# A recurrent trunk on one core: the RWKV's four steps written ahead of the HGRN's heads

## Chip, core and metric

The kernel runs on 1 core of one Trainium2 chip. The metric is the device time of one execution in microseconds (us); lower is better.

## What is computed

One layer of a streaming encoder on 256 frames of 1024 features: a layer norm, one wide projection, three mixers on slices of it, a gated merge, a layer norm, a mixture of experts, a layer norm.

```python
feats = h @ w_in
z, xbc, dt_raw, f_rwkv, f_hgrn, gates = _split(feats, IN_SIZES)
y_a = _ssd(z, xbc, dt_raw, ...)
y_b = _rwkv7(f_rwkv, ...)
y_c = _hgrn2(f_hgrn, ...)
merged = (sigmoid(g_a) * (y_a @ w_br_ssd) + sigmoid(g_b) * (y_b @ w_br_rwkv)
          + sigmoid(g_c) * (y_c @ w_br_hgrn))
h = _layernorm(DN_ALPHA * h + merged @ w_out, ln1_g, ln1_b)
h = _layernorm(DN_ALPHA * h + _moe(h, ...), ln2_g, ln2_b)
```

The two mixers of this change are recurrences over the frames. The RWKV-7 keeps a 64 by 64 state for each of 16 heads: `s = s * w_t + (s a_t) b_t + v_t k_t`, and gives `y = s r_t`, which is normed per head. The HGRN2 has 8 heads with a decaying outer-product state, computed in chunks of 64 frames, and a root-mean-square norm per head.

## The kernel before

**Projections.** `feat` (through `stream`, whose products stand on lines 358 to 368) makes 256 columns of `h @ w_in`. It loads two tiles of 512 KB, splits each weight into a high and a low part (`L183` on ScalarE, `L184` on VectorE, four buffers each), and issues 48 products into a PSUM tile `st` of three buffers: `L366` to `L368` with the weights stationary, `L358` to `L360` with the frames stationary. These 48 are called streams here. A stream waits for its split weights and its `st` tile, for nothing else.

**The RWKV.** `rwkv_part` prepares eight pairs of heads in two batches, `s0` (pairs 0 to 3) and `s1` (pairs 4 to 7). `rwkv_solve` inverts small triangular systems on VectorE, 32 times a product `L593` and a sum `L595`, and passes the result through DRAM (`L599`, `L605`). `rwkv_solve_off` completes the inverse: transposes `L618` on VectorE, products `L623`, copies `L627`, products `L631`, copies `L635`. Then four steps follow, each over two pairs of a batch. A step is `rwkv_b`, four rounds, one for each chunk of 64 frames:

```python
nc.tensor.matmul(ch[hs[h], 0, :], sc[:, h, c, 0:64], uv[:, c, h, :], ...)        # L654
nc.tensor.matmul(ch[h, 0, :], ars[h, c - 1, 0:64], z[h, c - 1, h], ...)          # L658
nc.scalar.activation(w, ch[:, 0, :], AF.Copy)                                    # L660
nc.tensor.matmul(ch[h, 1, :], tt[h, (i0 + f) * 4 + c, :], w[h], ...)             # L662
nc.scalar.activation(uv[hs[0], c, 0, :], ch[hs[0], 1, :], AF.Copy)               # L663, L665
nc.tensor.matmul(ch[hs[h], 2, :], bkt[:, c, hs[h]], uv[:, c, h, :], ...)         # L670
nc.vector.scalar_tensor_tensor(z[h, c, h], z[h, c - 1, h], pe[h, c - 1:c], ch[h, 2, :], ...)  # L676
```

The first round has no `L658` (and a copy, `L674`, for `L676`), the fourth no `L670`. After the rounds come the output products `L687` and `L691`, the norm on VectorE and ScalarE (`L694` sums, `L697`, `L702`, `L703` squares, `L705`, `L706`, the reciprocal root in `rsqrt`, lines 160 to 177, and `L708`), and `rwkv_out`: `L715`, transposes `L717`, `L722` on ScalarE, `L723` on GpSimd, `L724` on VectorE. The state `z`, the buffers of the norm and the two PSUM tiles `ch` are shared by the steps, so a step begins when the step ahead of it has read its `ch` tiles.

**The HGRN.** `hgrn(j)` handles heads 2j and 2j+1 (called head j here): three projections (q, v, gate, each kept in a ring of two buffers), scans `L859`, exponentials `L867` to `L870`, products `L879`, transposes `L885`, a copy `L887`, states `L893`, `L896`, `L899`, outputs `L905` and `L909`, squares `L913`, the root, the scaling `L917`, transposes `L920` and `L921`. It draws PSUM tiles from the pool `pmm` (three buffers), as `rwkv_solve_off` does, and the root's scratch tiles `rs_t`, `rs_z` (two buffers) from the same pool as the RWKV's norm.

**What sets the order.** `mixers` calls these functions, and the Tile scheduler makes one in-order queue for each engine out of them: an instruction that is emitted earlier has the higher priority, and one that is ready in the scheduler's own clockwork may go ahead of an earlier one that isn't. Buffers of pools are waited for as written. Behind the mixers come the gates' projections, the Mamba part (`ssd_prep`, `ssd`), the three branch products, and the experts. Parts of these are pulled forward by the scheduler: `L1021` (GpSimd broadcasts of a small table into the arena, read by `L1024`, `L1030` and `L1032` on ScalarE), and the start of the second layer norm's residual (`L1114` and `L1155`, loads issued by ScalarE; `L1152` on GpSimd; `L1156` and `L1157` on VectorE).

The arena is one SBUF tile whose places are used several times. Pairs 4 and 5, read last by the third step's products, lie where `L1114` loads its rows; pairs 6 and 7, read last by the fourth step's, lie where `L1021` and `L1030` write.

Of the kernel before, what the change touches and what calls it, by code (L numbers as in the profile page):

```python
# [139 lines left out]
class Kern:  # L140
# [585 lines left out]
    def mixers(self):  # L726

        self.pe = self.c1.tile([128, 8, 4], F32, name="pe")
        self.rwkv_lora()
        s0, s1 = self.rwkv_batch_start(0), self.rwkv_batch_start(1)  # L730
        self.later = []
        MARK('rwA0')
        self.rwkv_part(0, 0, s0)
        self.rwkv_part(0, 1, s0)
        MARK('rwA1')
        self.rwkv_part(1, 0, s1)
        if not SLATE:
            MARK('rwS0')
            with self.tc.high_priority(offset=PSV):
                self.rwkv_solve(0, s0)  # L740
            MARK('rwA1')
        exp = self.ssd_dt_start()
        self.rwkv_part(1, 1, s1)
        self.flush()
        if SLATE:
            MARK('rwS0')
            self.rwkv_solve(0, s0)
        self.rwt.release()
        self.ycp = self.open_("ycp", side="right")
        self.yc = self.ycp.tile([128, KT, L], F32, name="yc")  # L750
        self.hrp = self.open_("hrp", side="right")
        self.hr = Arena(self.hrp.tile([128, 33 * 256], F32, name="hr"))
        self.hgrn_bounds()
        self.hgrn_start()
        MARK('forget')
        self.hgrn_forget(exp)
        self.ssd_dt()
        MARK('rwS')
        self.rwkv_solve_off(s0)
        MARK('rwS1')  # L760
        with self.tc.high_priority(offset=PSV):
            self.rwkv_solve(1, s1)
        for j in range(4):
            if j == 2:
                MARK('rwS')
                self.rwkv_solve_off(s1)
            MARK('rwB%d' % j)
            self.rwkv_b(2 * (j % 2), (s0, s1)[j // 2])
            for i in (0, 1):
                self.rwkv_out(2 * (j % 2) + i, (s0, s1)[j // 2])  # L770
            MARK('hgrn%d' % j)
            self.hgrn(j)
        MARK('gates')
        self.gates(range(NG - NZ - NY))
        self.dump("dbg_yb", self.yb)
        self.dump("dbg_yc", self.yc)
        self.hrp.release()
# [966 lines left out]
```

## Time and profile before

| | |
|---|---|
| three runs, us | 815.62, 814.69, 813.25 (median 814.69) |
| profiled execution, us | 813.39, span 811.6 |
| mean granted TensorE clock | 0.983 |
| busy: TensorE, VectorE, ScalarE, GpSimd | 777.7, 513.1, 369.0, 137.7 us |
| HBM read | 180.13 MB, 225 GB/s over the span |

Times in rows are in us from the span's start, unless marked ns. PE is TensorE's matmul, PEld its weight load, DVE VectorE, ACT ScalarE, POOL GpSimd, SP the queue that issues most loads. PEclk is the granted TensorE clock as a share of 2.4 GHz. In a timeline row stand start, duration, engine, line, operation, output and input with their shapes, the number of instructions merged, and in brackets the idle time ahead of it with what ended it. An fp32 product leaves two records. A busy TensorE need not be at its peak, since products overlap and their ends are modelled.

### The profile page before, as it was taken

The page shows a single profiled execution, that of the slowest core. Times are in us where ns is not written, and L with a number is a line of the kernel's source. Part 1 is how long each engine was busy: PE and PEld are TensorE (multiplying, and loading weights), DVE is VectorE, ACT ScalarE, POOL GpSimd, SP SyncE. Part 2 cuts the span into 40 slices and gives each one's busy share as a digit, 9 for nine tenths or more (in the row PEclk, how much of TensorE's full clock was granted, in tenths as well). Part 3 has the DMA queues.
Part 4 walks back from the last instruction along what each step waited for, and adds up shares of the span by engine and source line. Part 5 has one row for each costly group of instructions (what it writes and reads, how often), then busy time and mean ns, then how long its engine had stood idle before and what let it go on. Part 6 is the DMA issues. An engine that isn't in the chain of part 4 may idle for free. (4 is left out here: it accounts for less than half of the span.)

```text
span 811.6 us, 16395 instructions
## 1 busy us (share of the span) xinstructions
PE 777.7 (96%) x6306; PEld 598.9 (74%) x6306; DVE 513.1 (63%) x1166; ACT 369.0 (45%) x817; POOL 137.7 (17%) x211
## 2 busy tenths in 40 slices
PE   7999999999999999999998999999999999999991
PEld 5898899988997998998797999999444434443440
DVE  6897899999987555576589897785612211221146
ACT  4765555575446555645486764452512121211111
POOL 3364633631002002010012111000000000001201
PEclk9999999999999999999899999999999999999995
DMA  7544555493463463565188579995999999999961
GB/s 236 173 126 117 115 144 138 137 215 103 131 151 111 130 182 107 147 195 178 45 270 305 163 221 277 328 313 177 368 386 387 387 386 386 387 388 385 387 229 55
DMA packets 146493, 183.92 MB, mean 227 GB/s; under 512 B 25561, under 2 KB 94440, under 8 KB 146408
## 3 DMA queue, kind: packets, MB, share of 16 engines
q1 hardware_dynamic: 142888, 176.91, 66.5%
q0 software_dynamic: 1472, 3.21, 1.6%
q10 hardware_dynamic: 2048, 2.70, 1.1%
q8 instruction: 51, 0.84, 0.4%
q14 instruction: 34, 0.28, 0.1%
HBM read 180.13 MB, written 2.65 MB: 225 GB/s over the span
## 5 line engine op out<-in xcount | busy, mean ns | idle before, releaser
L184 DVE TENSOR_TENSOR wlo<-raw,whi 128x512 fp32r<-128x512 f32 x268 | 190.2, 720 | 75.2 <-ACT whi L183 64.1
L183 ACT ACTIVATE whi<-raw 128x512 fp32r<-128x512 f32 x268 | 165.0, 623 | 152.7 <-PE st L367 117.3
L366 PE MATMUL st<-hhi,whi 128*128 128x256 f32 (+1 forms) x744 | 209.6, 289 | 2.4 <-ACT arena L784 1.4
L368 PE MATMUL st<-hhi,wlo 128*128 128x256 f32 (+1 forms) x744 | 210.5, 292 | 0.8 <-DVE wlo L184 0.8
L367 PE MATMUL st<-hlo,whi 128*128 128x256 f32 (+1 forms) x744 | 207.8, 287 | 0.0
L368 PEld LDWEIGHTS st<-hhi,wlo 128*128 128x128 f32 (+1 forms) x744 | 139.4, 191 | 8.5 <-issue 3.9
L366 PEld LDWEIGHTS st<-hhi,whi 128*128 128x128 f32 (+1 forms) x744 | 140.0, 191 | 7.3 <-issue 2.4
L367 PEld LDWEIGHTS st<-hlo,whi 128*128 128x128 f32 (+1 forms) x744 | 139.7, 191 | 2.7 <-issue 1.4
L1455 PE MATMUL b<-arena,xg 128*64 128x512 f32 x288 | 78.8, 596 | 0.0
L367 PE MATMUL st<-ylo,whi 128*128 128x256 f32 x192 | 52.5, 284 | 1.9 <-DVE ylo L184 1.9
L366 PE MATMUL st<-yhi,whi 128*128 128x256 f32 x192 | 53.0, 284 | 0.3 <-ACT whi L183 0.2
L368 PE MATMUL st<-yhi,wlo 128*128 128x256 f32 x192 | 52.1, 283 | 0.0
L1455 PEld LDWEIGHTS b<-arena,xg 128*64 128x64 f32 x288 | 23.8, 137 | 38.0 <-issue 34.5
L1528 DVE SCALAR_TENSOR_TENSOR elo<-b,egs,ehi 128x512 fp32r<-128x512 f32 x15 | 11.2, 750 | 60.7 <-ACT ehi L1527 60.7
L1508 PE MATMUL b<-arena,ehT 128*64 128x512 f32 x144 | 43.0, 596 | 0.0
L367 PEld LDWEIGHTS st<-ylo,whi 128*128 128x128 f32 x192 | 35.5, 189 | 2.6 <-DVE ylo L184 2.3
L1497 ACT ACTIVATE ehT<-b 128x256 f32<-128x256 f32 x16 | 6.2, 390 | 68.1 <-PE b L1496 68.1
L366 PEld LDWEIGHTS st<-yhi,whi 128*128 128x128 f32 x192 | 35.7, 189 | 0.8 <-ACT whi L183 0.4
L1489 DVE SCALAR_TENSOR_TENSOR ehi<-ehi,b 128x256 f32<-128x256 f32 x16 | 6.0, 418 | 47.0 <-PE b L1455 47.0
L368 PEld LDWEIGHTS st<-yhi,wlo 128*128 128x128 f32 x192 | 35.4, 189 | 0.2 <-issue 0.2
L593 DVE TENSOR_TENSOR arena<-arena 128x1 f32<-128x1 f32 (+15 forms) x64 | 33.1, 517 | 1.0
L1370 POOL TENSOR_TENSOR arena<-arena 128x512 f32<-128x512 bf16 x4 | 4.5, 1156 | 171.6 <-PE b L1455 171.6
(453 smaller groups left out, 1432.2 us busy)
## 6 DMA issues: line engine op xcount, KB each, us to landing
raw<-in_w_in_dram SPq DMA_DIRECT2D x102, 512.0 KB, 3.7
arena<-in_exp_w_gate_dram SPq DMA_DIRECT2D x40, 512.0 KB, 10.7
arena<-in_exp_w_down_dram SPq DMA_DIRECT2D x34, 512.0 KB, 10.8
arena<-in_exp_w_up_dram SPq DMA_DIRECT2D x32, 512.0 KB, 10.8
xsl<-in_exp_w_up_dram SPq DMA_DIRECT2D x32, 512.0 KB, 10.8
xsl<-in_exp_w_down_dram SPq DMA_DIRECT2D x20, 512.0 KB, 10.8
xsr<-in_exp_w_gate_dram SPq DMA_DIRECT2D x16, 512.0 KB, 10.7
raw<-in_w_br_rwkv_dram SPq DMA_DIRECT2D x8, 512.0 KB, 4.2
```

Source lines behind the costliest of these rows:

```text
L183: nc.scalar.activation(hi, raw, AF.Copy)
L184: nc.vector.tensor_tensor(lo, raw, hi.bitcast(F32), op=OP.subtract)
L366: nc.tensor.matmul(o, hi[:, kq, fs], xhi[:, k, :], start=st and f == 0, stop=False)
L367: nc.tensor.matmul(o, hi[:, kq, fs], xlo[:, k, :], start=False, stop=False)
L368: nc.tensor.matmul(o, lo[:, kq, fs], xhi[:, k, :], start=False, stop=sp and f == nf - 1)
L593: nc.vector.tensor_tensor(po, tu[:, :n, :t + 1], eu[:, :t + 1, t][:, None, :].to_broadcast([128, n, t + 1]), op=OP.mult)
L1370: nc.gpsimd.tensor_tensor(o, x[1], x[2], op=OP.add)
L1455: nc.tensor.matmul(ps[hs[e]], xg[:, k, hs[e]], W[nm, e, k // 2][:, k % 2, :], start=k == 0, stop=k == KT - 1)
L1489: nc.vector.scalar_tensor_tensor(th[:, c], th[:, c], 0.5, q["pu"][:, c], op0=OP.mult, op1=OP.mult)
L1497: nc.scalar.activation(q["hT"][:, 2 * j:2 * j + 2], tp, AF.Copy)
L1508: nc.tensor.matmul(pd[hs[e], :], q["hT"][:, k, hs[e]], W["exp_w_down", e, (n, k // 2)][:, k % 2, :], start=k == 0, stop=k == 3)
L1528: nc.vector.scalar_tensor_tensor(lo, pd, q["gs"], hi.bitcast(F32), op0=OP.mult, op1=OP.subtract)
```

## The change

Before, step j of the RWKV was written directly ahead of head j of the HGRN. After it, all four steps are written first, with the second solve's products (`rwkv_solve_off(s1)`) still ahead of the third step, and then the four heads.

```diff
         with self.tc.high_priority(offset=PSV):
             self.rwkv_solve(1, s1)
-        for j in range(4):
+        def rw(j):
             if j == 2:
                 MARK('rwS')
                 self.rwkv_solve_off(s1)
@@ -768,8 +768,14 @@
             self.rwkv_b(2 * (j % 2), (s0, s1)[j // 2])
             for i in (0, 1):
                 self.rwkv_out(2 * (j % 2) + i, (s0, s1)[j // 2])
+
+        def hg(j):
             MARK('hgrn%d' % j)
             self.hgrn(j)
+        for j in range(4):
+            rw(j)
+        for j in range(4):
+            hg(j)
         MARK('gates')
```

No instruction is added or taken away. From line 774 on, a line of the changed kernel has a number that is higher by 6, and so it is printed in the order's rows of the change; everywhere else in this text the lines are those of the kernel before.

**TensorE, end of the second step.** In the kernel before (numbers of buffers printed; `st` rows are streams):

```order
L687 MATMUL ch_2841<-arena_75 64x64 x8
L691 MATMUL ch_2841<-arena_75 64x128 x3
L687 MATMUL ch_2842<-arena_75 64x64 x8
L691 MATMUL ch_2842<-arena_75 64x128 x3
L366 MATMUL st_4479<-hhi_88,whi_4486 128x256
L368 MATMUL st_4409<-hhi_88,wlo_4451 128x256
L367 MATMUL st_4479<-hlo_89,whi_4486 128x256
```

And in the changed kernel, from the second step's fourth round to the third step's first product:

```order
L662 MATMUL ch_2544<-arena_75 64x64 x2
L662 MATMUL ch_2545<-arena_75 64x64 x2
L687 MATMUL ch_2544<-arena_75 64x64 x8
L691 MATMUL ch_2544<-arena_75 64x128 x3
L687 MATMUL ch_2545<-arena_75 64x64 x8
L691 MATMUL ch_2545<-arena_75 64x128 x3
L715 MATMUL ch_2685<-arena_75 128x256
L715 MATMUL ch_2692<-arena_75 128x256
L717 MATMUL ch_2685<-ident_98,arena_75 128x128 x2
L717 MATMUL ch_2692<-ident_98,arena_75 128x128 x2
L654 MATMUL ch_2771<-arena_75 64x64 x2
```

Before, 34 streams follow the output products and 49 more stand around `L715`; now none does. The last stream stands five groups ahead of these rows, the next one behind the fourth step, its `L717` and head 1's `L893`.

**VectorE, norm of the third step.** In the kernel before:

```order
L694 TENSOR_REDUCE gmean<-ch 128x4 x2
L697 TENSOR_SCALAR gmean<-gmean 128x8
L931 SCALAR_TENSOR_TENSOR arena<-st,hcw,arena 128x255
L702 TENSOR_TENSOR arena<-ch,gmean 128x256 x2
L931 SCALAR_TENSOR_TENSOR arena<-st,hcw,arena 128x254
L184 TENSOR_TENSOR wlo<-raw,whi 128x512
L931 SCALAR_TENSOR_TENSOR arena<-st,hcw,arena 128x253
L705 TENSOR_REDUCE gvar<-arena 128x8
L1156 SCALAR_TENSOR_TENSOR arena<-arena,li_mv 128x1024 x2
```

And in the changed kernel:

```order
L694 TENSOR_REDUCE gmean<-ch 128x4 x2
L1162 SCALAR_TENSOR_TENSOR arena<-arena,li_mv 128x1024 x2
L697 TENSOR_SCALAR gmean<-gmean 128x8
L702 TENSOR_TENSOR arena<-ch,gmean 128x256 x2
L705 TENSOR_REDUCE gvar<-arena 128x8
L706 TENSOR_SCALAR gvar<-gvar 128x8
L160 TENSOR_SCALAR gr_y<-gvar 128x8
L1163 SCALAR_TENSOR_TENSOR arena<-arena,ln_r_y 128x1024 x2
L165 TENSOR_TENSOR rs_t<-gr_y 128x8
```

The residual's operation (1156 before, 1162 now) moves from behind the sum of squares to ahead of the mean.

**ScalarE, end of the fourth step.** In the kernel before (`L183` splits weights for streams, `L1056` belongs to the Mamba part):

```order
L703 ACTIVATE arena<-arena 128x256 x2
L932 ACTIVATE arena<-arena 128x256
L183 ACTIVATE whi<-raw 128x512
L1056 ACTIVATE arena<-st 128x256
L1030 ACTIVATE arena<-arena,sdT 128x128 x8
```

And in the changed kernel (`L923` is `L917` of before for head 0, `L893` is `L887` for head 1):

```order
L703 ACTIVATE arena<-arena 128x256 x2
L1036 ACTIVATE arena<-arena,sdT 128x128 x8
L1038 ACTIVATE arena<-arena 128x1024
L923 ACTIVATE hr<-mm,hr_y 128x128 x4
L722 ACTIVATE arena<-ch,par 128x256 x2
L1030 ACTIVATE arena<-arena 128x1024
L1036 ACTIVATE arena<-arena,sdT 128x128 x8
L893 ACTIVATE hr<-mm 128x512
L858 ACTIVATE hr<-st 128x512
```

The Mamba tables' operations have kept their place behind this step; the HGRN's heads 0 and 1 now stand among and behind them, and the splits for streams are gone from between.

## Rows read from the trace of the kernel before

**Rows 1.** The page, busy us with share of the span and instructions:

```profile
PE 777.7 (96%) x6306; PEld 598.9 (74%) x6306; DVE 513.1 (63%) x1166; ACT 369.0 (45%) x817; POOL 137.7 (17%) x211
```

**Rows 2.** Busy time by stretch: length, engines' busy us, PEclk, DMA share, GB/s:

```profile
182.50:512.00 329.50, 321.75 (x3100) 292.50 (x3100) 245.43 (x569) 188.63 (x451) 37.36 (x38) 0.99 0.57 173
421.00:512.00 91.00, 87.36 (x753) 83.28 (x751) 79.18 (x166) 58.40 (x122) 14.20 (x16) 1.00 0.79 250
580.00:785.00 205.00, 205.00 (x1226) 86.31 (x1224) 45.17 (x108) 37.52 (x85) 8.95 (x8) 1.00 1.03 381
```

**Rows 3.** Timeline of PE, streams with a group between them:

```profile
402.31 0.28 PE L366 MATMUL st<-hhi,whi 128*128 128x256 f32 x1
402.43 0.28 PE L367 MATMUL st<-hlo,whi 128*128 128x256 f32 x1
402.64 0.33 PE L662 MATMUL ch<-arena 64*64 64x64 f32 x4
402.90 0.39 PE L368 MATMUL st<-hhi,wlo 128*128 128x256 f32 x1
403.12 0.28 PE L366 MATMUL st<-hhi,whi 128*128 128x256 f32 x1
```

**Rows 4.** Timeline of PE, fourth step, rounds without streams and the return:

```profile
387.70 0.34 PE L654 MATMUL ch<-arena 128*64 128x64 f32 x4
387.96 0.33 PE L658 MATMUL ch<-arena 64*64 64x64 f32 x4
...
389.58 0.45 PE L662 MATMUL ch<-arena 64*64 64x64 f32 x8 [0.76 <-ACT arena L660]
...
391.59 0.34 PE L654 MATMUL ch<-arena 128*64 128x64 f32 x4 [0.32 <-DVE arena L676]
...
393.87 1.10 PE L670 MATMUL ch<-arena 128*64 128x64 f32 x8
394.90 0.58 PE L366 MATMUL st<-hhi,whi 128*128 128x256 f32 x1
...
398.70 0.38 PE L368 MATMUL st<-hhi,wlo 128*128 128x256 f32 x1
```

**Rows 5.** Busy time by stretch, the clock in these rounds:

```profile
392.00:394.00 2.00, 1.83 (x22) 1.27 (x22) 1.97 (x6) 0.84 (x5) 0.00 (x0) 0.52 0.29 98
```

**Rows 6.** Timeline of PE, the third step's output products and the next stream:

```profile
352.25 0.69 PE L687 MATMUL ch<-arena 128*64 128x64 f32 x16
...
354.21 0.39 PE L368 MATMUL st<-hhi,wlo 128*128 128x256 f32 x1
```

**Rows 7.** Timeline of DVE, the third step's norm:

```profile
355.31 0.74 DVE L702 TENSOR_TENSOR arena<-ch,gmean 128x256 f32<-128x256 f32 x2
...
358.56 2.48 DVE L1156 SCALAR_TENSOR_TENSOR arena<-arena,li_mv 128x1024 f32<-128x1024 f32 x2 [0.53 <-DMA arena<-in_ln_in_g_dram]
...
363.76 2.47 DVE L1157 SCALAR_TENSOR_TENSOR arena<-arena,ln_r_y 128x1024 f32<-128x1024 f32 x2
```

**Rows 8.** Timeline of ACT, operations of the steps' ends:

```profile
411.94 0.71 ACT L703 ACTIVATE arena<-arena 128x256 f32<-128x256 f32 x2
...
415.15 2.45 ACT L1030 ACTIVATE arena<-arena,sdT 128x128 f32<-128x128 f32 x8 [1.41 <-DMA arena<-acsd]
...
418.82 1.05 ACT L1032 ACTIVATE arena<-arena 128x1024 f32<-128x1024 f32 x1
```

**Rows 9.** Answers on single lines: POOL's L723 and L1152, landing of L1021's loads:

```profile
L723 POOL TENSOR_TENSOR arena<-arena x8: 723/742/1384, 247.3 to 426.0; 128x256 f32<-128x256 f32 x8
L1152 POOL TENSOR_SCALAR arena<-arena x1: 3764/3764/3764, 359.9 to 359.9; 128x1024 f32<-128x1024 f32 x1
DMA to landing us min/median/max: 4.6/6.3/7.2
```

**Rows 10.** Timeline of DVE, end of the second solve and its return from DRAM:

```profile
233.86 0.69 DVE L595 TENSOR_REDUCE arena<-arena 128x16 f32<-128x512 f32 x1
...
242.19 1.43 DVE L618 STREAM_TRANSPOSE arena<-arena 32x512 f32<-32x512 f32 x2 [2.27 <-DMA arena<-td]
```

## The prediction, made before the change was run

> **What bounds the kernel now.** I read the page first: over the span of 811.6 us TensorE is busy for 777.7 us, 96%, more than any other engine [rows 1]. The execution took 813.39 us, so 1.8 us lie around the span; the median of the three runs, 814.69 us, is 1.3 us above it. My sum is made against 813.4.
>
> The second view is the busy time by stretch. From 182.5 us, where the program order first changes, to 512 us, the end of the last Mamba group, TensorE is busy for 321.75 of 329.5 us at a granted clock of 0.99 [rows 2]. So this stretch ends when TensorE has worked through its queue, and time in which it stands still there goes straight to the end. After it the experts move 381 GB/s for 205 us [rows 2]; the change leaves their code alone, so I let that stage move as a block.
>
> The third view is TensorE's timeline. Its bulk are the streamed projections, products of 256 columns that wait for nothing but the next weight tile: one every 0.12 us (402.31, then 402.43). Each visit of another kind costs some 0.2 us beyond its own work: 0.21 us to the first `L662`, and 0.22 us instead of 0.12 after the return [rows 3].
>
> The RWKV is the opposite. One step is a chain of four rounds, each TensorE, ScalarE, TensorE, ScalarE, TensorE, VectorE. A group of four records (two fp32 products) takes 0.26 us (387.70 to 387.96), so a full round of eight groups is 2.1 us of TensorE work. At one place, from 387.7 to 394.9 us, the program of before has no stream to put between the groups, and one sees what a bare round costs: 3.9 us (387.70 to 391.59), then 3.4 us (391.59 until `L670` ends at 394.97), with waits of 0.76 us on ScalarE and 0.32 on VectorE among them [rows 4]. In 392 to 394 us, after those waits, the clock is granted at 0.52, the 1.2 GHz level; the streams that return at 394.90 come every 0.21 us until 398.70 [rows 4, 5]. Elsewhere some twenty streams (2.4 us) follow a group, and the chain's latency costs nothing.
>
> **What the change moves.** (Lines are those of the kernel before.) By the rows of the order, the HGRN's first head can no longer finish between the steps: its first products stand behind the second solve's `L631`, and its scaling by the root, `L917`, stands on ScalarE behind the fourth step's `L703`. My reading is that tiles of a pool are given out in the order of emission, and these share pools with the RWKV. The projections have two buffers each for q, v and gate, so with head 0 unfinished only heads 0 and 1 can be streamed. Counted in the TensorE order from the first `L631` on, 381 stream products stand ahead of the end of the fourth step; before, 1259 did. They run out ahead of the second step's fourth round. From there to the first stream behind the fourth step TensorE has only the bare chain. I price that stretch piece by piece.
>
> *Rounds.* Four full ones (second and third round of steps three and four) at 3.4 us, the value at the lower clock, since TensorE will often wait: 13.6. Two first rounds lack the two `L658` groups and the wait for the state, 2.9 each: 5.8. Three fourth rounds end with the second `L665`, 2.3 each: 6.9. Together 26.3 us.
>
> *Output products* `L687`, `L691`: 2.0 us a step at full clock (352.25 to 354.21) [rows 6], at most 4.0 at half; I take 2.6, as they are many small ones: three times, 7.8 us.
>
> *Norm and output of the second step*, from the last `L691` to the next step's first product [rows 7 to 9]: seven operations of VectorE (`L694`, `L697`, `L702`, `L705`, `L706`, `L708`, `L724`), of which the `L702` pair, 0.74, is the longest, 3.3 us in all; the root's ten short ones 1.7; ScalarE's second `L703` and one and a half `L722`, of 256 columns like the 0.71 pair, 1.2; the first transposes 0.4; `L723` 0.74; and some 0.1 for each of ten handovers: 8.3 us.
>
> *The same of the third step* has passengers. Both `L1156` now stand on VectorE right behind `L694`, ahead of `L697`. They need a row loaded by `L1114`, which may start only when the step's products have read that place in the arena; before, `L1156` began at 358.56, 4.4 us behind the end of those products, having waited for this load [rows 6, 7]. So `L697` comes at 4.4 + 2.5 = 6.9 instead of 0.5 us. Both `L1157` stand behind `L160` and take 2.5; they need GpSimd's `L1152` of 3.76 us, and began at 363.76 before, 9.5 us behind the products [rows 7, 9], which is when `L160` will be through. The tail is 8.3 + 6.4 + 2.5 = 17.2 us.
>
> *Behind the fourth step* ScalarE's order puts eight `L1030` (2.45 us [rows 8]) and `L1032` (1.05 [rows 8]) ahead of head 0's `L917`, then `L722`, `L1024` (of 1024 columns like `L1032`), eight more `L1030`, and only then `L887`, which head 1's products `L893` need; and these stand ahead of the first stream. Each set of eight waits for a 512 KB broadcast issued by GpSimd, the second one once the first set has freed the buffer. Landing took 4.6 to 7.2 us [rows 9]; I take 4.6, as the streams' loads stand still then. From the last `L691`: landed at 4.8, eight done at 7.3, second landing 12.0, `L1024` 13.1, eight done 15.5, and about 2.5 for `L887` and the products: 18 us. The Trainium skill, DMA: Bandwidth & Descriptors, section on the anatomy of one DMA on the gpsimd path, gives a fixed 2.0 us plus bytes by 436 GB/s, an estimate of 3.2 us for 512 KB; with it the sum would be 2.8 us smaller, but no landing here was below 4.6.
>
> The bare stretch is 26.3 + 7.8 + 8.3 + 17.2 + 18 = 78 us. Of this TensorE would have worked anyway 16.4 us in rounds (four of 2.1, five of 1.6), three times 3.1 for output products and transposes, and some 3.3 for the two heads: 29 us. **New idle time: 49 us.**
>
> *Smaller terms.* The second solve's `L623` now stands ahead of the third step's products and of the streams that follow. `L618`, which it needs, began 7.7 us behind the last `L595` (234.55 to 242.19, waiting for a load) [rows 10]. VectorE will be through the solve some 7 us earlier, since by the order 17 operations of mostly 0.4 to 0.7 us leave it; so `L618` starts near 235 and `L623` near 237. TensorE is there earlier: 285 streams are 34.2 us, the first step 10.5, 21 visits 4.2, that is 231.4. About 4 us are lost, with groups that come late 2 to 8. After the bare stretch streams begin at 1.2 GHz (1.6 us over 18 of them [rows 4]) and ScalarE has head 1's exponentials ahead of the splits: 4 us for both, 2 to 6. In return losses of before go: 1.1 us of waits and 1.6 us of slow streams [rows 4], and 19 visits fewer (66 runs of streams by the order, 85 before) at 0.2 us: 7 us.
>
> **Sum: 49 + 4 + 4 - 7 = 50 us slower**, 813.4 + 50 = 863 us for a profiled execution; the median stood 1.3 us higher before, so 864 us.
>
> **The rivals.** *The rounds are cheaper.* If TensorE keeps 2.4 GHz and the other engines, now empty, answer at once, full rounds take 2.6, first ones 2.2, fourth ones 1.8, output products 2.0 and the tails 7.5, 16 and 16: 66 us bare, 37 idle, with +4 +2 -7 it is 36 us, 850. For it speaks that part of the 3.9 us was ScalarE finishing other work; against it the 0.52 in the second round.
>
> *They are dearer.* With 3.9, 3.4 and 2.8 us for the rounds, output products at half clock and loads at 7.2 us, tails of 9.5, 19 and 23: 94 us bare, 65 idle, with +5 +6 -7 it is 69 us, 883.
>
> *Faster.* VectorE may be the hidden bound: it is busy for 79.18 of 91 us in 421 to 512 [rows 2]. Had TensorE as much time to spare there as the bare chain costs, the chain done early would cost nothing and the 7 us of losses would come back: 807 us. This decides once TensorE's idle time in 182.5 to 512 reaches 49 us; it is 7.75 [rows 2].
>
> *The order does not take effect*, because the scheduler goes by readiness: 813 to 815 us. The rows of the order show the groups moved.
>
> **How the numbers follow.** Forecast 0.62, cheaper 0.17, dearer 0.18, faster 0.02, no effect 0.01. So faster 0.02, same 0.01, slower 0.97; 0.3%, 2.4 us, is about what a measurement of this kernel can tell from no change. The range takes in most of the cheaper and the dearer case: 844 to 886 us.
>
> **What would show it.** In the profile after: a stretch of 70 to 90 us from about 265 us without a stream product, with long waits of TensorE and the clock near 0.5; full rounds of 3 to 4 us; `L1156` between `L694` and `L697` with a wait on a load; a gap of over 10 us ahead of head 1's `L893`; the experts' 205 us unchanged. Wrong would be streams inside that stretch, less than 35 us of idle time in it, or a later stage that gives the time back.

## The result, and the profile after

The changed kernel takes 866.51 us (median of four runs, 865.51 to 867.26) against 814.02 us before: ratio 1.0641, 95% interval 1.062 to 1.0663. The forecast was 864, in a range of 844 to 886. The profiled execution took 866.73 us, 53.3 us more than that of before.

The page, with busy time and the slices of TensorE and its clock (compare [rows 1]):

```profile
PE 799.9 (92%) x6306; PEld 616.0 (71%) x6306; DVE 515.3 (60%) x1166; ACT 370.6 (43%) x817; POOL 136.5 (16%) x211
PE   7999999999899746899999989999999999999991
PEclk9999999999959556799999999999999999999996
```

The same work keeps TensorE busy 22 us longer, and a hole stands in slices 14 to 17. The clock is down there, and in slice 12 too. On TensorE's timeline these are the last stream ahead of the hole and the first one behind it; no stream stands between them:

```profile
274.46 0.28 PE L360 MATMUL st<-whi,hlo 128*128 128x256 f32 x1
...
353.06 0.58 PE L366 MATMUL st<-hhi,whi 128*128 128x256 f32 x1
```

Busy time by stretch:

```profile
182.50:512.00 329.50, 292.99 (x2658) 259.26 (x2657) 204.98 (x480) 163.73 (x402) 28.45 (x32) 0.87 0.45 132
236.00:265.00 29.00, 27.55 (x288) 22.11 (x289) 12.20 (x29) 12.83 (x37) 3.47 (x4) 0.59 0.13 38
274.70:353.10 78.40, 46.63 (x450) 33.70 (x449) 32.04 (x105) 27.75 (x93) 11.58 (x13) 0.61 0.27 84
286.90:303.20 16.30, 14.74 (x156) 10.85 (x156) 4.62 (x16) 5.15 (x24) 0.80 (x3) 0.52 0.14 46
303.20:318.20 15.00, 3.25 (x11) 1.92 (x10) 10.25 (x22) 1.80 (x4) 4.47 (x3) 0.59 0.39 126
318.20:334.10 15.90, 14.43 (x156) 10.60 (x156) 3.97 (x14) 5.16 (x24) 0.15 (x1) 0.53 0.10 20
334.10:353.10 19.00, 8.25 (x51) 5.98 (x49) 6.81 (x31) 11.99 (x30) 4.97 (x6) 0.66 0.36 116
353.10:566.40 213.30, 211.07 (x1777) 200.73 (x1776) 152.26 (x322) 122.17 (x257) 17.82 (x18) 0.99 0.62 194
182.50:566.40 383.90, 345.73 (x3112) 310.40 (x3111) 248.73 (x573) 191.15 (x453) 34.88 (x38) 0.88 0.50 151
632.00:837.00 205.00, 205.00 (x1226) 86.29 (x1224) 44.86 (x110) 38.49 (x88) 8.95 (x8) 1.00 1.04 385
```

In 182.5 to 512 us TensorE is now busy for 293 us where it was for 322 [rows 2]. The third row is the stretch without a stream, 78.4 us; the four below it are the third step's rounds and output products, its tail, the fourth step's rounds and output products, and what stands behind them. After it TensorE is full again, and the experts take their 205 us [rows 2]. Hardly anything is given back: the last Mamba group ended at 512 before and ends at 567 now, and the whole execution is 53.3 us longer.

The loss has two parts. From 182.5 us to about the end of the last Mamba group TensorE was busy for 321.75 of 329.5 us before [rows 2] and is busy for 345.73 of 383.9 now. So it stands still for 38.2 us instead of 7.75, some 30 us more, and needs 24 us more for the same work, since much of it runs at 1.2 GHz (granted clock 0.88 over this stretch, 0.99 before).

TensorE's timeline of a full round in the third step (its first groups, and the start of the next round):

```profile
290.20 0.48 PE L654 MATMUL ch<-arena 128*64 128x64 f32 x4 [0.17 <-DVE arena L674]
290.62 0.48 PE L658 MATMUL ch<-arena 64*64 64x64 f32 x4
...
291.70 1.01 PE L662 MATMUL ch<-arena 64*64 64x64 f32 x8
292.68 1.07 PE L670 MATMUL ch<-arena 128*64 128x64 f32 x8
293.92 0.48 PE L654 MATMUL ch<-arena 128*64 128x64 f32 x4 [0.17 <-DVE arena L676]
```

A full round takes 3.7 us, and there is hardly a wait in it (0.17 us). A group of four that took 0.34 us [rows 4] takes 0.48 at this clock, and groups follow each other every 0.41 us instead of 0.26: most of the round is TensorE's own products at 1.2 GHz, not the handovers.

VectorE in the third step's norm, and ScalarE behind the fourth step (compare [rows 7, 8]; L1162 and L1163 are L1156 and L1157 of before):

```profile
303.37 0.42 DVE L694 TENSOR_REDUCE gmean<-ch 128x4 f32<-128x256 f32 x1 [0.72 <-PE ch L691]
305.29 2.48 DVE L1162 SCALAR_TENSOR_TENSOR arena<-arena,li_mv 128x1024 f32<-128x1024 f32 x2 [1.50 <-DMA arena<-in_ln_in_g_dram]
307.69 1.00 DVE L697 TENSOR_SCALAR gmean<-gmean 128x8 f32<-128x8 f32 x1
...
311.03 2.48 DVE L1163 SCALAR_TENSOR_TENSOR arena<-arena,ln_r_y 128x1024 f32<-128x1024 f32 x2
...
314.82 0.69 DVE L708 TENSOR_TENSOR arena<-arena,gr_y 128x512 f32<-128x512 f32 x1
```

```profile
339.01 2.45 ACT L1036 ACTIVATE arena<-arena,sdT 128x128 f32<-128x128 f32 x8 [2.41 <-DMA arena<-acsd]
341.49 1.06 ACT L1038 ACTIVATE arena<-arena 128x1024 f32<-128x1024 f32 x1
342.57 1.14 ACT L923 ACTIVATE hr<-mm,hr_y 128x128 f32<-128x128 f32 x4
...
346.51 1.06 ACT L1030 ACTIVATE arena<-arena 128x1024 f32<-128x1024 f32 x1 [1.88 <-DMA arena<-acsd]
347.47 2.43 ACT L1036 ACTIVATE arena<-arena,sdT 128x128 f32<-128x128 f32 x8
349.81 0.58 ACT L893 ACTIVATE hr<-mm 128x512 f32<-128x512 f32 x1
```

Both are as forecast: the norm stands still for a load and for five us of the residual; both sets of the Mamba tables (L1036, L1030 of before) and their loads stand ahead of L893, for which the first stream waits.

TensorE's waits in 230 to 362 us (total, times, longest):

```profile
PE ch L717 <- DVE arena L708: 10.2, 3, 4.2
PE ch L715 <- DVE arena L702: 9.0, 3, 6.0
PE mm L899 <- ACT hr L893: 4.2, 1, 4.2
...
PE mm L623 <- DVE rs_t L166: 3.3, 1, 3.3
```

The norms are behind the first two, the tables behind the third, and the second solve's products now wait 3.3 us from 233 us (and 0.8 more for L618). For the 3.3 us the profile names L166, but the first L618, which these products need too, had itself waited for its load from DRAM and began at 235.8 us.

### The profile page after: what moved, and what is told of

It reads as the page before. It is cut to its first block, busy times and chain, and to the rows that moved or that the text cites. A ratio compares the mean times of both kernels' runs of the same rounds, so it can differ in the third digit from the quotient of the medians.

```text
span 864.9 us, 16437 instructions
## 1 busy us (share of the span) xinstructions
PE 799.9 (92%) x6306; PEld 616.0 (71%) x6306; DVE 515.3 (60%) x1166; ACT 370.6 (43%) x817; POOL 136.5 (16%) x211
## 5 line engine op out<-in xcount | busy, mean ns | idle before, releaser
L183 ACT ACTIVATE whi<-raw 128x512 fp32r<-128x512 f32 x268 | 165.3, 624 | 155.1 <-PE st L367 118.6
L184 DVE TENSOR_TENSOR wlo<-raw,whi 128x512 fp32r<-128x512 f32 x268 | 188.2, 709 | 70.7 <-ACT whi L183 63.4
L1088 POOL TENSOR_TENSOR arena<-arena 128x256 f32<-128x256 f32 x8 | 8.4, 1045 | 153.5 <-DVE arena L1086 148.5
## 6 DMA issues: line engine op xcount, KB each, us to landing
arena<-in_exp_w_down_dram SPq DMA_DIRECT2D x34, 512.0 KB, 10.8
arena<-in_exp_w_up_dram SPq DMA_DIRECT2D x32, 512.0 KB, 10.8
xsl<-in_exp_w_up_dram SPq DMA_DIRECT2D x32, 512.0 KB, 10.8
xsr<-in_exp_w_gate_dram SPq DMA_DIRECT2D x16, 512.0 KB, 10.8
```

The source lines that it names most:

```text
L183: nc.scalar.activation(hi, raw, AF.Copy)
L184: nc.vector.tensor_tensor(lo, raw, hi.bitcast(F32), op=OP.subtract)
L1088: nc.gpsimd.tensor_tensor(y, y, zz, op=OP.mult)
```

## The experiments

All start from the changed kernel. Ratios are to the kernel before, run on the same chips beside them; its medians there were 813.8 us (experiments 1, 6, 7, 9), 814.8 (2 to 5) and 812.6 (8, 10).

**1. Scratch of the HGRN's own for the root.**

```diff
-        t = pool.tile([128, 8], F32, name="rs_t")[:, :shape[1]]
-        z = pool.tile([128, 8], F32, name="rs_z")[:, :shape[1]]
+        own = "h" if name == "hr" else ""
+        t = pool.tile([128, 8], F32, name=own + "rs_t")[:, :shape[1]]
+        z = pool.tile([128, 8], F32, name=own + "rs_z")[:, :shape[1]]
```

> The changed kernel, with scratch tiles of the HGRN's own for its reciprocal root (names of their own in the same pool), nothing else. Theory A (the loss is the bare chain, and the chain is bare because the HGRN's root gets its scratch behind the fourth step's, so that head 0 stays unfinished and the projections run out of buffers): heads finish between the steps, streams stand between the rounds again, the stretch of 78 us without a stream is gone, and the time falls from 866.5 to 812 to 826 us (likeliest 818: before plus some 4 us for the wait of the second solve's products, which still stand ahead). Rival B (the PSUM tiles that the heads share with the second solve hold head 0, not the scratch): still a bare stretch of over 50 us and at least 850 us. Rival C (the passengers, residual and Mamba tables, are what costs): they still stand where they were, so at least 845 us.

Measured: 823.46 us, ratio 1.0108 (1.0071 to 1.0145), in theory A's range, 5.5 us above its likeliest value. Two names bring back 43 of the 52.5 us. Its busy time by stretch shows no hole, and where the rest went:

```profile
230.00:240.00 10.00, 6.07 (x100) 5.04 (x98) 5.17 (x17) 2.96 (x6) 0.25 (x1) 0.82 0.67 151
240.00:250.00 10.00, 9.94 (x124) 7.61 (x122) 3.81 (x13) 3.50 (x11) 1.16 (x2) 0.50 0.16 54
250.00:260.00 10.00, 10.00 (x55) 7.88 (x56) 5.72 (x16) 5.68 (x19) 2.06 (x2) 0.50 0.00 0
...
300.00:350.00 50.00, 50.00 (x461) 41.15 (x460) 27.60 (x75) 27.65 (x81) 5.42 (x7) 1.00 0.36 109
```

TensorE waits 3.9 us for the second solve's products at 232 to 236 us, and then works for 20 us at 0.50 of the clock. From 260 to 350 us it is full.

**2. Four buffers for the shared scratch** (`bufs=4` for `rs_t` and `rs_z`, names as before).

> The changed kernel, with four buffers in place of two for the root's scratch rs_t and rs_z, still shared by the RWKV and the HGRN. Theory A (a pool's tiles are given out in the order of emission, however many there are): the instructions stand as in the changed kernel, the stretch of 78 us stays, 864 to 869 us. Rival F (two buffers were too few: the head's root waited for the buffer that the third step's root had): with four it would take the first step's, long free; 815 to 830 us as with scratch of its own.

Measured: 863.99 us, a single run, at the lower edge of theory A's range. The instructions stand in the order of the changed kernel, and the stretch without a stream is there with the same length:

```profile
272.30:351.00 78.70, 47.70 (x449) 34.35 (x448) 31.66 (x105) 27.66 (x93) 12.24 (x13) 0.59 0.26 82
```

Buffers were not short. What fits this and the two names is that tiles of one name are given out in the order in which they are written in the program: head 0's root is written behind the fourth step's, and so it stands behind it.

**3. Heads 0 and 1 ahead of the second solve's products**, shared scratch.

```diff
-        for j in range(4):
-            rw(j)
-        for j in range(4):
-            hg(j)
+        for f, j in ((rw, 0), (rw, 1), (hg, 0), (hg, 1), (off, 0), (rw, 2), (rw, 3), (hg, 2), (hg, 3)):
+            f(j)
```

(`off` is `rwkv_solve_off(s1)`, taken out of `rw`; its number is not used.) This also moves the roots of heads 0 and 1 ahead of those of steps three and four.

> The changed kernel with its shared scratch, but head 0 and head 1 written ahead of the second solve's products: steps 1 and 2, heads 0 and 1, products, steps 3 and 4, heads 2 and 3. Theory A: only the second step is bare (head 0's root is still behind the second step's), some 24 us by the measured pieces (rounds 12, output products 2.7, tail 8 to 9) with 10 us of full-clock work in it, and the wait of the products falls away, so about 14 us above before: 822 to 836 us, likeliest 828. Rival G (any step that is not followed by its own head costs what it cost in the changed kernel, some 17 us a step for three steps): over 840 us.

Measured: 829.68 us, ratio 1.0195 (1.0154 to 1.0235), 1.7 us from theory A's likeliest value. The last stream ahead of the second step ends at 249.9 us, the next one begins at 274.4: 24.5 us, with 24 expected. The clock in its bare rounds:

```profile
250.00:252.00 2.00, 1.11 (x20) 0.69 (x20) 0.90 (x2) 1.63 (x7) 0.00 (x0) 1.00 0.81 235
252.00:254.00 2.00, 1.69 (x24) 1.16 (x24) 0.89 (x4) 0.49 (x3) 0.00 (x0) 0.91 0.86 260
254.00:260.00 6.00, 5.21 (x50) 3.54 (x52) 2.17 (x8) 2.16 (x11) 0.00 (x0) 0.50 0.04 14
```

**4. Both together.** With scratch of its own, the loops of before and the order of experiment 3 give the same order of instructions on every engine (by rows of the order that are not shown here); it was run in the loops of before.

> The order of the kernel before (each step followed by its head, the products ahead of the third step), with scratch of the HGRN's own. Its instructions stand in the same order as those of the changed loops (two steps, two heads, products, two steps, two heads) with that scratch, so one run stands for both. Theory A: where the root's scratch is not shared, the order of writing steps and heads costs nothing, and the bare rounds of before at 388 to 395 us (some 4 us lost) are filled: 806 to 815 us. Rival I (the shared scratch also kept the heads from crowding VectorE and ScalarE, so that freeing it costs more than it gives in this order): 816 to 825 us.

Measured: 816.14 us, ratio 1.0017 (0.9996 to 1.0038): no difference that can be told from before. By the time alone it lies just above theory A's 806 to 815 us, at the bottom of rival I's 816 to 825. Of theory A the first half holds within that interval, that this order of writing costs nothing then; its gain of some 4 us did not come, and rival I is not excluded. Together the experiments make a square (us):

| | products ahead of the heads | behind heads 0 and 1 |
|---|---|---|
| shared scratch | 866.5 | 829.7 |
| own scratch | 823.5 | 816.1 |

Either half alone takes back most of the loss, and with the scratch freed the place of the products is still worth 7 us. That the scratch holds head 0 is shown. With shared scratch the second column moves the roots too, so the square doesn't show a second cause by itself; that head 0 also waits for the PSUM tiles that it shares with the second solve's products is argued from the program. Tiles of its own there were not tried.

**5. Own scratch, products behind head 0 alone** (two steps, head 0, products, two steps, three heads).

> Scratch of the HGRN's own as in the first experiment, and the second solve's products written behind head 0: steps 1 and 2, head 0, products, steps 3 and 4, heads 1 to 3. Theory A: what the first experiment still lost against before (9.7 us) lies at 230 to 260 us of it: 3.9 us of waits of the second solve's products and 20 us at a granted clock of 0.50, since head 0 could not start ahead of them. Both fall away, so 13 us or so are gained against 823.5, and the time is 806 to 814 us. Rival H (the rest of the loss is spread over more visits between streams and rounds): 818 to 826 us.

Measured: 822.41 us, ratio 1.0102 (1.007 to 1.0134). It fails theory A's 806 to 814 us and lies in rival H's range. Busy time by stretch:

```profile
230.00:260.00 30.00, 29.60 (x387) 27.11 (x383) 19.64 (x46) 15.15 (x32) 2.21 (x3) 1.00 0.60 159
350.00:380.00 30.00, 28.26 (x262) 26.50 (x261) 21.94 (x45) 14.14 (x30) 4.02 (x4) 1.00 0.70 222
380.00:410.00 30.00, 26.43 (x237) 23.11 (x236) 16.54 (x37) 13.76 (x38) 0.52 (x1) 0.89 0.31 93
```

The wait and the low clock at 230 to 260 us did go. But TensorE now stands still for 5.3 us at 350 to 410 (1.0 in experiment 1), half of it ahead of streams that wait for ScalarE and half in handovers of a step, with the clock down to 0.89 in the last 30 us. TensorE is busy for 782.7 us over the span, 777.7 before [rows 1]; from the first solve's products to the last transposes of the Mamba part its trace has 106 runs of streams where that of before has 84, which at 0.2 us a visit is an estimate of 4.4 us. So rival H describes it better: what a better place brought in one stretch went to another, and, by the estimate, to visits.

**6. The residual's loads held back**, so that L1162 and L1163 leave the third tail.

```diff
-        g, b = self.bcast_row(0, "ln_in_g"), self.bcast_row(1, "ln_in_b")
+        with self.tc.issue_after(self.hold_act.ins):
+            g, b = self.bcast_row(0, "ln_in_g"), self.bcast_row(1, "ln_in_b")
```

(`hold_act` is the scaling by the root, L923, of the last head.)

> The changed kernel, with the loads of the residual's start held back behind the scaling of the last head, so that L1162 and L1163 leave the third step's norm. Theory A with the measured third tail (15.0 us against 7.9 of the second): the tail becomes 8 to 9 us, the bare stretch 71 to 73, the time 859 to 862 us. Rival C (passengers are the larger part of the loss, since each delays a whole chain): under 850 us. Rival D (the tail is as long without them, because ScalarE's and GpSimd's part sets it): 865 to 868 us.

Measured: 862.13 us, ratio 1.0584 (1.0545 to 1.0624), 0.1 us above theory A's range; the tail is not as long without them, as rival D had it. The tail from the last L691 to the next L654 on TensorE:

```profile
301.29 0.60 PE L691 MATMUL ch<-arena 128*64 128x128 f32 x5
303.23 1.10 PE L715 MATMUL ch<-arena 128*128 128x256 f32 x4 [1.34 <-DVE arena L702]
307.24 0.66 PE L717 MATMUL ch<-ident,arena 128*128 128x128 f32 x4 [2.90 <-DVE arena L708]
309.59 0.48 PE L654 MATMUL ch<-arena 128*64 128x64 f32 x4 [1.70 <-DVE arena L724]
```

7.7 us from 301.9 to 309.6, as long as the second step's (7.9 in the changed kernel), and 71.7 us without a stream. The stretch is 6.7 us shorter, the time only 4.4; where the rest went is not shown.

**7. The tables' loads held back** (`issue_after` on the last head's subtraction on GpSimd, around the load of L1027, the L1021 of before).

> The changed kernel, with the loads of the Mamba tables held back behind the HGRN's last head, so that both sets of L1036 leave ScalarE behind the fourth step. Theory A with the measured 19.0 us from the last output product to the first stream: without the two sets and their loads some 9 us are left, and the time is 855 to 859 us, unless the tables come too late for the Mamba part (then up to 866). Rival C: under 850 us.

Measured: 859.03 us, ratio 1.0551 (1.0505 to 1.0596), at the upper edge of theory A's range. On ScalarE no L1036 is left behind the fourth step:

```profile
338.60 1.14 ACT L923 ACTIVATE hr<-mm,hr_y 128x128 f32<-128x128 f32 x4 [2.83 <-DVE hr_y L177]
341.48 1.02 ACT L722 ACTIVATE arena<-ch,par 128x256 f32<-128x256 f32 x2 [1.74 <-PE ch L717]
343.00 0.60 ACT L858 ACTIVATE hr<-st 128x512 f32<-128x512 f32 x1 [0.50 <-DVE yc L927]
```

The first stream comes at 343.65, 9.9 us behind the fourth step's output products instead of 19.0. The stretch without a stream is 71.0 us.

**8. Both held back.**

> The changed kernel, with the residual's and the tables' loads both held back. Theory A (each tail is a piece of one serial stretch, so the gains add): 866.5 less 4.4 and 7.5, what each gave alone, so 853 to 856 us, and the ten rounds in a row without a stream stay. Rival C (with both gone the rest of the stretch collapses): under 845 us. Rival J (they overlap, the longer gain alone counts): 858 to 860 us.

Measured: 855.77 us, ratio 1.0541 (1.0499 to 1.0583), in theory A's range. The stretch is 63.2 us; alone the two shorten it by 6.7 and 7.4, so 64.3 was to be expected of one serial chain:

```profile
272.80:336.00 63.20, 42.83 (x448) 31.36 (x448) 26.26 (x100) 19.88 (x74) 5.58 (x9) 0.70 0.13 40
```

Against the kernel before on the same chips the loss falls from 52.5 to 43.2 us. So the passengers are some 9 us of it, give or take 4 by the two intervals, less than the 15.2 us by which the stretch shrank.

**9. Filler for TensorE.** The new kernel does more work: products of the identity's 128 columns with 64 columns of `uv`, into unused columns of the steps' PSUM tiles, read by nobody.

```diff
+    def fill(self, bank, uv, c, n):
+        for _ in range(n):
+            self.nc.tensor.matmul(bank[:, 448:512], self.ident, uv[:, c, 0, :], start=True, stop=True)
```

(one for each pair behind L660's place and behind L662's in rounds two to four of steps two to four, 40 behind each of these steps' output products)

> The changed kernel with more work: products into an unused part of the steps' PSUM tiles, two at each handover of a round in steps two to four, and 40 behind the output products of each, which nobody reads. Theory A (latency of the chain sets the bare rounds; the clock is second): full rounds stay at 3.3 to 3.8 us or grow, the time is 866 to 880 us. Rival E (the low clock is what makes the bare chain long: in the rounds TensorE was busy for 14.7 of 16.3 us at 0.52): with TensorE kept busy the clock in the rounds of steps three and four rises to over 0.9, full rounds fall to 2.3 to 2.9 us although they hold more work, output products from 2.7 to 2.0, and the time is 850 to 862 us.

Measured: 901.36 us, a single run, outside both ranges, so as a test of the clock's price it is void: the 40 took 9.1 us, longer than the wait they were to fill. It still shows this (a full round of the third step, and the filler behind that step):

```profile
301.00:307.00 6.00, 5.70 (x40) 4.27 (x40) 1.02 (x5) 1.32 (x6) 0.00 (x0) 0.50 0.00 0
321.60:324.00 2.40, 2.37 (x21) 2.37 (x22) 0.21 (x1) 0.00 (x0) 0.00 (x0) 1.00 0.78 229
```

With TensorE busy for 5.7 of 6 us the rounds still got 0.50, and grew from 3.7 to 6 us by the filler's own time. Rival E's remedy doesn't work with this filler; how long the chain would be at full clock stays open, but for one round: in experiment 3 the first round, entered at full clock, took 2.7 us (249.9 to 252.6), in the changed kernel 3.3.

**10. Two tries at a better kernel.** In the loops of before, with both loads held back:

> The order of the kernel before, with the residual's and the tables' loads held back as in the experiment ahead. Theory A (what stands between two steps costs only where no stream covers it): before, only the rounds at 388 to 395 us are bare, and with the loads held back the order puts 48 streams there; that gives back some 3 to 5 us, so 808 to 812 us. Rival K (in the order of before these operations are covered wholly, and the bare round cost nothing): 813 to 816 us. Rival L (the tables come late for the Mamba part, which then waits): 817 to 825 us.

Measured: 818.26 us, ratio 1.0064 (1.0043 to 1.0085), slower by 0.4 to 0.9%. Two rows, the stretch of the bare rounds of before and the one behind it, and below them the second one in the kernel before:

```profile
380.00:410.00 30.00, 28.87 (x303) 25.34 (x303) 19.84 (x51) 18.24 (x53) 0.97 (x1) 1.00 0.47 149
410.00:440.00 30.00, 20.83 (x142) 18.73 (x142) 25.98 (x59) 19.00 (x47) 6.03 (x5) 0.79 0.89 292
...
410.00:440.00 30.00, 26.62 (x220) 25.00 (x219) 27.29 (x68) 25.75 (x63) 5.71 (x6) 1.00 0.88 292
```

The first is as theory A has it: clock 1.00, where before had 0.52 at 392 to 394 [rows 5]. But in the second TensorE stands still for 9.2 us, 3.4 before; 5.8 of them are waits of the Mamba part's products. The time is rival L's. That the late tables are the cause is shown in part: the profile puts 1.0 us of these waits down to an operation on the tables (L1039) itself.

Each head written ahead of its step (head 0, step 1, head 1, step 2, products, head 2, step 3, head 3, step 4), shared scratch:

> Shared scratch, and each head written ahead of its step: head 0, step 1, head 1, step 2, products, head 2, step 3, head 3, step 4. Theory A: no round is bare (8 to 95 streams a round by the order), which saves the 3 to 5 us that before loses at 388 to 395, but streams and other work change places 14 times more often, at 0.2 us each 3 us: 811 to 817 us. Rival M (heads in front hold the steps back, and the Mamba part starts later): 819 to 830 us.

Measured: 816.63 us, ratio 1.0041 (1.002 to 1.0061). It lies in theory A's range, at the upper end, and is 0.2 to 0.6% slower than before. No version here beats the kernel before.

## Why the prediction was right, point by point

- **That head 0 stays unfinished and the streams run out**: shown, by the stretch of 78.4 us and by experiments 1 to 3. The scratch's order of writing, only argued then, fits the four buffers, which left the order as it was, and the two names, which brought back 43 of the 52.5 us. A hold by the PSUM tiles, the other half of that reading, stays argued.
- **The bare stretch**, 78 us forecast, 78.4 measured, from pieces that partly cancel:

| piece | forecast | measured |
|---|---|---|
| rounds | 26.3 | 28.7 |
| output products | 7.8 | 7.8 |
| second step's tail | 8.3 | 7.9 |
| third step's tail | 17.2 | 15.0 |
| behind the fourth step | 18 | 19.0 |

 The sum is nearer than its pieces, so part of this is luck. The rounds were dearer: 3.7 us for a full one, not 3.4, and 3.3 for a first one, not 2.9. In steps three and four the clock was at 0.50 in all of them. The 3.4 had been read at a round whose first two groups still ran at full clock, and only until the end of L670, without the handover to the next round; from start to start the rounds here take 3.7. The third tail was shorter because L1162's load came sooner (it began 2.1 us behind the products, not 4.4) and GpSimd's L1158, 3.2 us from 307.2, was done when L1163 was due (7.8 us behind the products, not 9.5). The broadcasts of L1027 landed in 4.5 to 5.5 us, 4.6 forecast. The Trainium skill, DMA: Bandwidth & Descriptors, section on the anatomy of one DMA, gives a fixed 2.0 us plus bytes by 436 GB/s, an estimate of 3.2 us for 512 KB. No landing here shows that.
- **"New idle time: 49 us"** is right as a loss and wrong as idle time. In the stretch TensorE is busy for 46.6 of 78.4 us and idle for 31.8, less than the 35 us that the prediction named as a sign of being wrong. The difference is the clock: work that it counted as 29 us takes 46.6, since most of it runs at 1.2 GHz. The price of the pieces had the half clock in it, the split did not. Another sign came only in part: no single wait there is over 10 us. Ahead of head 1's products it is 4.2 us, and all waits between the fourth step's output products and the first stream add up to 10.8.
- **Its start**, about 265 us forecast, was 274.7: the first stretch up to there ran slower, see the next point.
- **The second solve's products**: 3.3 and 0.8 us of waits, 4 forecast. What the step "about 4 us are lost, with groups that come late 2 to 8" left out is the clock: at 236 to 265 us 0.59 was granted, and the streams among the second step's first rounds came at half speed (24 in 5.2 us). By an estimate from that row, 27.55 us of work at 0.59, this is some 11 us of TensorE's time that the sum didn't have. Experiment 1 has the same stretch; in experiment 5 it was gone, and only 1 us was gained, so its price is not shown by a run.
- **The sum**: 53.3 us more than before. The first L623 came 1.8 us later already, ahead of any change; the stretch less the forecast 29 us of work is 49.4, the wait 4.1; so the rest, the half clock of 236 to 265, the return and the losses of before that went, comes to -2.0 net, where +4 and -7 were forecast. That the half clock, which was not in the sum, did not push the total further off is luck: these smaller terms cancel, and they are not told apart by a run.
- **The rivals**: the cheaper rounds at full clock did not occur. "Faster", VectorE as the hidden bound, would have needed time to spare on TensorE; 353 to 566 us is busy for 211.07 of 213.3. That the order takes no effect is out by the rows.

## What to carry to other kernels

When a long chain of small dependent products lives in the gaps of a stream of independent ones, the question for any reordering is not how much work it moves but whether the stream can still advance: look for every buffer that the stream's consumers share with the chain, scratch of a few bytes included, and for the order in which its tiles are given out. A name of its own for eight columns of scratch was worth 43 us here, and four buffers under the shared name next to nothing (864.0 us in one run, against 866.5). A stretch that goes bare also pulls work of other stages into its path, and such a passenger then lengthens it (by 6.7 and 7.4 us here; without them the total fell by 4.4 and 7.5), while covered by streams it is sometimes, as the passengers of experiment 10, better left where it is.

## What had not been expected of the hardware

- The granted clock stayed at the lower level in rounds with hardly a wait. In experiment 3 TensorE stood still for 0.89 of 2 us and for 0.31 of the next 2; in the second of these the clock fell, and it was 0.50 for the 6 us behind them, with TensorE busy for 5.21. In the filled rounds of experiment 9 it was 0.50 with TensorE busy for 5.70 of 6, and in the run of independent products behind that step (2.37 of 2.40) it was 1.00.
- The filler's fp32 products of 64 columns, with weights of 128 columns, came at 0.114 us a record at full clock (80 records in 9.14 us), about the 0.12 us of a stream of 256 columns [rows 3]; in that run the weight loads were busy for 2.37 of 2.40 us, as long as the products. The rounds' products of 64 columns, whose weights have 64 columns, came at 0.065 (four records in 0.26 us).
